# A decoder trunk on one core: the activation of a pass's last unit moved to VectorE, the residual prepared behind its read-back, output products in single steps, and more turned K tiles

## The chip, the core and the metric

The kernel runs on one core of a Trainium2 chip. The core has a matrix engine (TensorE, "PE" in the profile; its weight loads are "PEld"), a vector engine (VectorE, "DVE"), an activation engine (ScalarE, "ACT"), GpSimd ("POOL", used here to issue a few transfers) and SyncE ("SP", which issues all weight loads). The metric is the device time of one execution in microseconds.

## The reference

Two decoder layers over 256 positions of width 2048, in float32. Layer 0 mixes with a gated short convolution, layer 1 with multi-head latent attention; both are followed by the same kind of MLP, and every sub-layer ends in a normalisation of a scaled residual:

```python
def sq_relu_mlp(x, w1, w2):
    return jnp.square(jax.nn.relu(x @ w1)) @ w2

    for layer in range(DEPTH):                       # DEPTH = 2, N_A = 1
        if layer < N_A:
            mix = short_conv_mixer(h, ...)
        else:
            mix = mla_mixer(h, ...)                  # 16 heads, then o @ w_o
        h = layer_norm(ALPHA * h + mix, ...)
        h = layer_norm(ALPHA * h + sq_relu_mlp(h, mlp_w1[layer], mlp_w2[layer]), ...)
```

The MLPs (2048 to 8192 and back) are most of the arithmetic, and the change lies mainly in them.

## The kernel before

**Numbers in two parts.** Each float32 operand is split into hi and lo, both in the matrix engine's fast 32-bit type, and a product is hi·hi + lo·hi + hi·lo. A weight tile is loaded as `raw` (512 KB, SyncE), ScalarE casts it to `hi` (line 136), VectorE subtracts to get `lo` (line 137). An activation tile holds its hi and lo halves side by side. So a product of one K tile is `high` (line 224: weight hi by 512 columns) and `low` (line 228: weight lo by 256 columns), and `whole` (lines 366 and 367) adds the two halves of the result: a copy on ScalarE, then an addition on VectorE. `mm_run` goes over the 16 K tiles in the order high, low; for the K tile numbered `turned` (2) it puts low ahead of high. `TURN(q, m)` says for which units that is done.

**The MLP in passes.** The 8192 hidden columns are done in eight passes `q` of 1024; a pass has eight units `m` of 128 columns (`ps_u`), each with all 16 K tiles. Passes 0 and 7 are plain. In passes 1 to 6 (`FAST`) the second matrix product uses seven products instead of eight on 2 by 2 blocks. Two units make a pair: their sums are written to the two halves of a tile `u` (`fp` in the profile), ScalarE applies Relu and Square to the whole of it once the second unit is there (line 730), `form` builds block sums in three VectorE instructions (lines 645, 646, 648), and a split (lines 136 and 137 again) writes the pair's left factors: `h1c` and `h1a` for the first MLP (pairs 0 and 1, and pairs 2 and 3 of a pass), `h3c` and `h3a` for the second. On the right, the weights of the second product are combined as well: `raw_t` (line 171) and two more instructions (175, 178) on VectorE make further tiles that are split like the rest.

**Order.** `steps` gives, per unit, the set of seven products (`ps`, 21 matmuls, lines 309, 311, 312) that follows it. It is delayed by `SHIFT` = 5 units: behind units 5, 6, 7 of a pass come the products of its pairs 0, 1, 2 with the first half of the outputs, behind unit 0 of the next pass those of pair 3, and then the four pairs with the second half. So the factors of pair 3, which need unit 7, are used after one more set of products and one more unit. When the first half is done, ScalarE copies seven sums out of the PSUM banks and seven others in (lines 620, 695).

**The residual.** `held_x` holds the input of the sub-layer. In the first MLP, `begin` prepares it for the next normalisation while pass 1 runs: chunk 0 behind half of pass 0's output blocks (`ps_d`), with a scaling (line 419), two matmuls that take its mean over the partitions (`mu0p`, line 421) and a copy; the other 15 behind units 0 to 4 of pass 1, one VectorE instruction each (line 426: scale, subtract). Each group of chunks is then written to DRAM (`parked`, line 738, five transfers from POOL's queue), since its place in SBUF is needed for `sums`. After pass 7's hidden units the chunks are read back (`xback`, line 761, four transfers), and `to_wide` adds the turned output blocks to them, counts the moments and casts (lines 512, 431 to 437, 453, 454) for the next products.

**The output projection of attention** starts while the last heads are still being finished: `out_first` issues the matmuls of three output blocks K tile by K tile, and `BEHIND` says how many of its steps follow each step of the heads.

**Who orders the work.** The code emits instructions in program order; a planner in the framework then fixes, when the kernel is built, the order of each engine's queue, by emission order and by when it estimates operands to be ready. In the trace an engine's order therefore differs from the order of emission: splits of later weights stand between instructions of one pair. Once fixed, each queue runs in order. Weights are prepared some steps ahead (`take`), in 7 raw buffers and 9 pairs of hi and lo.

Of the kernel before, what the change touches and what calls it, by code (L numbers as in the profile page):

```python
# [13 lines left out]
ALU = mybir.AluOpType  # L14
# [4 lines left out]
T = 256  # L19
D = 2048  # L20
NC = D // P
FF = 4 * D
NQ = 8
QC = FF // NQ // P
H = 16
# [9 lines left out]
NB = 4  # L35
BW = D // NB
FAST = range(1, NQ - 1)
SHIFT = 5


def TURN(q, m):
    return m == 0 or not (q == 1 and m < SHIFT or q == NQ - 1 and m > SHIFT)
FIRST = (0, 1, 2, 3, 4, 6, 8, 12, 16)
LEAD = 4
HEAD = 4
# [2 lines left out]
TURNED = 2  # L48
LAG = 8
WO_G = 3  # L50
BEHIND = (2, 2, 2, 3, 2, 2, 3)

C_G, C_B, C_CW, C_QG, C_KG, C_END = 0, 64, 128, 176, 180, 184

# [2 lines left out]
def trunk(ctx: ExitStack, tc: tile.TileContext, xT, vecs, lead, w_first, w_in, w_out, w_kv, w_q, w_uk, w_uv,  # L57
          w_qn, w_qp, w_o, w1, w2, w2f, cosT, sinT, mask, ident, gb, out):
    nc = tc.nc
# [11 lines left out]
    held_x = [xres]  # L71
    parked = ctx.enter_context(tc.tile_pool(name="parked", bufs=1, space=bass.MemoryType.DRAM)).tile(
        [P, NC, T], F32, tag="parked", name="parked")
# [136 lines left out]
    def psum(name, bank=None):  # L210

        bank = Banks.next() if bank is None else bank
        return (pmm if bank < 4 else Banks.more).tile([P, 512], F32, tag=f"mm{bank}", name=name)
# [8 lines left out]
    def high(ps, w, blk, x, first):  # L222

        nc.tensor.matmul(ps, w[blk // 8][0][:, blk % 8, :], x, start=first, stop=False)  # L224

    def low(ps, w, blk, x, last):

        nc.tensor.matmul(ps[:, :T], w[blk // 8][1][:, blk % 8, :], x[:, :T], start=False, stop=last)  # L228

    def mm_run(wps, x, k0, k1, nk, turned=None):  # L230

        for k, (w, ps) in [(k, u) for k in range(k0, k1) for u in wps]:
            if k == turned:
                low(ps, w, k, x[k], False)
            high(ps, w, k, x[k], k == 0)
            if k != turned:
                low(ps, w, k, x[k], k == nk - 1)
# [86 lines left out]
    def down(x, put, n, sums=None):  # L324

        ps = [sums[n, t] if sums else psum("ps_d") for t in range(2)]
        for j in range(len(x) // 2):
            w, = take(1)
            for kk in range(2):
                k = 2 * j + kk  # L330
                for t in range(2):
                    dot(ps[t], wide_rows(w, kk), held(x[k], t), k == 0 and not sums, k == len(x) - 1, onto=bool(sums))
        for t in range(2):
            put(n, t, ps[t])
# [190 lines left out]
    xhl = [t[:, k, :] for t in xts for k in range(NC // 2)]  # L525
# [17 lines left out]
    for k0, k1 in pieces:  # L543
        half, at = k0 // 8, slice(k0 % 8, (k1 - 1) % 8 + 1)
        xt = xts[half][:, at, :]
        x, w = sources[k0]
# [12 lines left out]
    for m in range(NC):  # L559
        part = []  # L560
        for what in "cub":
            ps = next(pss)
# [23 lines left out]
    def mlp(idx, ln, blocks, fast, begin=None, extra=None, last=False):  # L586
# [5 lines left out]
        xhl = [xt[:, k, :] for k in range(NC)]  # L592
# [57 lines left out]
        def finish_pair(j, u):  # L650
            f = factors[j // 2][:, j % 2]
            if q in FAST:
                form(u)
                split(f[:, 0, :], f[:, 1, :], u[:, P:])
            else:
                split(f[:, 0, :2 * T], f[:, 1, :2 * T], u[:, :2 * T])

        q = 0
        for m in range(QC):
            if m < GROUP:  # L660
# [5 lines left out]
                ps = ws[m][1]  # L666
            else:
                ws = [(take(), psum("ps_w"))]
                mm_wide(ws, ln.xd)
                ps = ws[0][1]  # L670
# [4 lines left out]
        acc = act.tile([P, 2, D], F32, tag="a1", name=f"acc{idx}")  # L675
        for n in range(NB):
            down(h, put, n)
            if begin and n == 1:
                begin(range(1), (Banks.count + 4) % 8)

        base = Banks.count
        bank = {p: (base + i) % 8 for i, p in enumerate(("6", "unit", "3", "1", "5", "7", "2", "4"))}
# [2 lines left out]
        ps, onto, fresh = {}, set(), set()  # L685
# [30 lines left out]
        for q, m, pair in steps():  # L716
            lone = pair is None
            if q == FAST[0] and m == SHIFT:
                for o, _, _ in FACTORS:
                    resume(o, 1)  # L720
            w = take(2, 7)
            at = "6" if lone and m % 2 == 0 else "unit"
            un = psum("ps_u", bank[at])
            mm_run([(w, un)], xhl, 0, NC, NC, turned=TURNED if TURN(q, m) else None)
            if m % 2 == 0:
                u = fast.tile([P, 8 * P], F32, tag="fp", name="fp")
            whole(un, u[:, (m % 2) * T:(m % 2 + 1) * T])
            if m % 2:
                for function in (AF.Relu, AF.Square):
                    nc.scalar.activation(u[:, :2 * T], u[:, :2 * T], function)  # L730
                if m > 1 or lone:
                    finish_pair(m // 2, u)
            if extra and q == FAST[0] and m < NB:
                for t in range(2):
                    extra(block, m, t, spare[1 + (2 * m + t) % 3])
            if begin and q == FAST[0] and m < SHIFT:
                begin(range(3 * m + 1, 3 * m + 4))
                nc.gpsimd.dma_start(parked[:, 3 * m + (m > 0):3 * m + 4, :], held_x[0][:, 3 * m + (m > 0):3 * m + 4, :])
            if q == FAST[0] and m == SHIFT:
                sums = act.tile([P, 4, 2, BW], F32, tag="xres", name=f"sums{idx}")  # L740
            if q == NQ - 1:
                for _ in range(3 if m >= SHIFT else 2):
                    next(folds, None)
            if pair:
                products_of(*pair)
            if m == 1 and not lone:
                finish_pair(0, u)
            if q == NQ - 1 and last and m >= QC - 2:
                for t in range(2):
                    last_sum(m - QC + 2, t, spare[2 * (m - QC + 2) + t])  # L750
# [14 lines left out]
    def to_wide(block, put, h):  # L765

        def turned(n):
            for c in range(2):
                ps = psum("turned")
                for j in range(4):  # L770
                    src = block(n, j % 2)[:, (2 * c + j // 2) * P:(2 * c + j // 2 + 1) * P]
                    nc.tensor.transpose(ps[:, j * P:(j + 1) * P], src, id_t)
                summed(ln, [ps[:, j * T:(j + 1) * T] for j in range(2)], add, 4 * n + 2 * c)

        ln.widen("b")
        for n in range(NB):
            down(h, put, n)
            if n:
                turned(n - 1)
        ln.ws = group_of(GROUP)  # L780
        mm_wide(ln.ws, ln.xd, 0, NC - 4)
        turned(NB - 1)
        mm_wide(ln.ws, ln.xd, NC - 4)
# [3 lines left out]
    def prepare_chunks(chunks, bank=None):  # L787
        for k in chunks:
            ln.prepare(k, bank)
# [5 lines left out]
    with tc.tile_pool(name="att", bufs=1) as ap:  # L795
# [68 lines left out]
        for m in range(NK):  # L864
            ps = next(pss)
# [16 lines left out]
        oT = [ot[:, k, :] for k in range(H)]  # L882
# [6 lines left out]
        with tc.tile_pool(name="att2", bufs=2) as a2, \  # L889
# [83 lines left out]
            first_o = []  # L973
            after = Norm(2, ALPHA)

            def out_first():

                for i in range(WO_G):
                    first_o.append((take(), psum("ps_wo")))
                for k in range(H):  # L980
                    mm_run(first_o, oT, k, k + 1, H)
                    after.prepare(k)
                    yield

            boxes = [{} for _ in range(4)]
            for _ in project(0, boxes[0]):
# [1 line left out]
            for g in range(1, 4):  # L988
# [5 lines left out]
                for _ in items:  # L994
                    pass
            outs = out_first()
            for s, n in enumerate(BEHIND, H - 4):
                together(s)
# [178 lines left out]
```

## Time and profile before

| | |
|---|---|
| median of 3 runs | 2008.79 us (2006.48 to 2009.18) |
| profiled execution | 2009.8 us, span 2007.7 us |
| TensorE busy | 1990.3 us (99%) |
| VectorE busy | 1719.5 us (86%) |
| ScalarE busy | 1291.6 us (64%) |
| mean granted TensorE clock | 0.998 |
| read from HBM | 383.87 MB |

The passes of the first MLP lie between about 380 and 1060 us of the span, those of the second between about 1330 and 1998. A timeline row is: start, duration, engine, line, operation, output and inputs, shapes, count, and in brackets the idle time of the engine ahead of it with what ended it. Durations of queued instructions overlap by some tenths of a microsecond, so the pace is read from the distance of starts. A row of the waits is: who waited for whom, total us, times, longest.

### The profile page before, as it was taken

The numbers are of one execution on the slowest core, as the hardware profiler recorded it, in microseconds if no ns is written. First come the engines' busy times: TensorE is split into PE (matmuls) and PEld (weight loads), VectorE is DVE, ScalarE is ACT, GpSimd is POOL, SyncE is SP. The second block draws the span as 40 slices with busy tenths as digits, with TensorE's granted clock in tenths as the row PEclk, the third lists the DMA queues.
The fourth block names the chain that finished last, engine by engine and source line by source line (L and its number), as shares of the span: only waits on it lengthen the run. The fifth ranks groups of instructions, "written<-read, shape, count | busy, mean of one in ns | idle before, by whom it ended". The sixth has DMA issues, their size and how long they took to land.

```text
span 2007.7 us, 29769 instructions
## 1 busy us (share of the span) xinstructions
PE 1990.3 (99%) x11062; PEld 1733.5 (86%) x11062; DVE 1719.5 (86%) x2493; ACT 1291.6 (64%) x1914; POOL 7.3 (0%) x30
## 2 busy tenths in 40 slices
PE   9999999999999999999999999999999999999998
PEld 8888888988888888888889998898888888888886
DVE  8667677798899999999988988778989999999995
ACT  7444445586667767677756655557676776767772
POOL 0000000000000000000000000000000000000000
PEclk9999999999999999999999999999999999999999
DMA  9666666575565565655764543656556556665572
GB/s 344 210 192 186 189 188 192 182 223 157 195 212 175 202 210 190 211 186 202 261 218 153 182 138 131 185 187 181 165 171 210 190 190 208 207 212 181 198 261 95
DMA packets 107888, 390.00 MB, mean 194 GB/s; under 512 B 12000, under 2 KB 12768, under 8 KB 107488
## 3 DMA queue, kind: packets, MB, share of 16 engines
q1 hardware_dynamic: 106560, 383.79, 58.8%
q0 software_dynamic: 1040, 4.19, 0.6%
q8 instruction: 86, 1.41, 0.3%
q14 instruction: 58, 0.48, 0.1%
q10 hardware_dynamic: 144, 0.13, 0.0%
HBM read 383.87 MB, written 4.19 MB: 193 GB/s over the span
## 4 chain that ended last, share of the span: by engine, by line
PE 87%; DVE 8%; issue 3%; DMA 1%; ACT 1%; DVEq 0%; ACTq 0%
PE ps_u L224 16%; PE ps_l L224 13%; PE ps_u L228 8%; PE ps_l L228 7%; PE ps L312 6%; PE ps L309 6%; PE ps L311 6%; DVE lo L137 3%; PE ps_d L309 2%; PE ps_d L312 2%; PE ps_d L311 2%; PE ps_w L258 2%; PE ps_w L257 2%; PE ps_w L256 2%; DVE raw_t L171 1%
## 5 line engine op out<-in xcount | busy, mean ns | idle before, releaser
L137 DVE TENSOR_TENSOR lo<-raw,hi 128x1024 fp32r<-128x1024 f32 x710 | 855.3, 1218 | 175.8 <-ACT hi L136 105.7
L136 ACT CAST hi<-raw 128x1024 fp32r<-128x1024 f32 x710 | 735.5, 1054 | 223.3 <-PE ps_l L224 103.6
L224 PE MATMUL ps_u<-xhl,hi 128*128 128x512 f32 x1792 | 620.6, 393 | 0.0
L228 PE MATMUL ps_u<-xhl,lo 128*128 128x256 f32 x1792 | 485.4, 280 | 0.0
L224 PEld LDWEIGHTS ps_u<-xhl,hi 128*128 128x128 f32 x1792 | 329.0, 187 | 66.5 <-issue 0.3
L228 PEld LDWEIGHTS ps_u<-xhl,lo 128*128 128x128 f32 x1792 | 338.0, 189 | 12.8
L224 PE MATMUL ps_l<-xhl_a,hi 128*128 128x512 f32 x704 | 244.1, 393 | 0.0
L228 PE MATMUL ps_l<-xhl_a,lo 128*128 128x256 f32 x704 | 195.4, 279 | 0.0
L136 ACT CAST hi_t<-raw_t 128x1024 fp32r<-128x1024 f32 x96 | 101.5, 1058 | 133.5 <-DVE raw_t L171 126.1
L224 PEld LDWEIGHTS ps_l<-xhl_a,hi 128*128 128x128 f32 x704 | 132.1, 188 | 29.9
L228 PEld LDWEIGHTS ps_l<-xhl_a,lo 128*128 128x128 f32 x704 | 131.9, 188 | 0.2
L171 DVE TENSOR_TENSOR raw_t<-raw,raw 128x1024 f32<-128x1024 f32 x96 | 116.8, 1217 | 10.6 <-DMA raw<-in_w2f_dram 10.6
L137 DVE TENSOR_TENSOR lo_t<-raw_t,hi_t 128x1024 fp32r<-128x1024 f32 x96 | 116.9, 1218 | 1.1 <-ACT hi_t L136 1.0
L366 ACT COPY t<-ps_u 128x256 f32<-128x256 f32 x112 | 41.5, 371 | 89.7 <-PE ps_u L228 89.5
L224 PE MATMUL ps_l<-z,hi 128*128 128x512 f32 x240 | 82.4, 391 | 0.0
L730 ACT ACTIVATE fp<-fp 128x512 f32<-128x512 f32 x112 | 71.5, 638 | 8.8 <-DVE fp L367 8.1
L258 PE MATMUL ps_w<-xd,hi 128*128 128x258 f32 x256 | 72.7, 284 | 0.0
L224 PE MATMUL ps_l<-oT,hi 128*128 128x512 f32 x208 | 72.6, 398 | 0.0
L256 PE MATMUL ps_w<-xd,hi 128*128 128x258 f32 x256 | 72.3, 282 | 0.0
L257 PE MATMUL ps_w<-xd,lo 128*128 128x258 f32 x256 | 72.3, 282 | 0.0
L178 DVE TENSOR_TENSOR raw<-raw 128x512 f32<-128x512 f32 x96 | 66.2, 690 | 2.4
L175 DVE TENSOR_TENSOR raw<-raw,raw_t 128x512 f32<-128x512 f32 x96 | 65.7, 684 | 1.0
(349 smaller groups left out, 3878.4 us busy)
## 6 DMA issues: line engine op xcount, KB each, us to landing
raw<-in_w_dram SPq DMA_DIRECT2D x320, 512.0 KB, 4.2
raw<-in_w2f_dram SPq DMA_DIRECT2D x192, 512.0 KB, 5.2
raw<-in_w_in_dram SPq DMA_DIRECT2D x88, 512.0 KB, 3.7
raw<-in_w_out_dram SPq DMA_DIRECT2D x32, 512.0 KB, 4.2
raw<-in_w_o_dram SPq DMA_DIRECT2D x32, 512.0 KB, 4.1
raw<-in_w_kv_dram SPq DMA_DIRECT2D x10, 512.0 KB, 4.4
raw<-in_w_q_dram SPq DMA_DIRECT2D x8, 512.0 KB, 4.0
raw<-in_w_uk_dram SPq DMA_DIRECT2D x8, 512.0 KB, 4.2
```

The source lines that it names most:

```text
L136: nc.scalar.copy(hi, src)
L137: nc.vector.tensor_tensor(lo, src, hi.bitcast(F32), ALU.subtract)
L171: nc.vector.tensor_tensor(t.rearrange(two, a=2), b12.unsqueeze(1).to_broadcast([P, 2, BW]), r1.rearrange(two, a=2), ALU.subtract)
L224: nc.tensor.matmul(ps, w[blk // 8][0][:, blk % 8, :], x, start=first, stop=False)
L228: nc.tensor.matmul(ps[:, :T], w[blk // 8][1][:, blk % 8, :], x[:, :T], start=False, stop=last)
L256: nc.tensor.matmul(ps[:, :W], hi, x[k][:, :W], start=k == 0, stop=False)
L257: nc.tensor.matmul(ps[:, :W], lo, x[k][:, :W], start=False, stop=False)
L258: nc.tensor.matmul(ps[:, :W], hi, x[k][:, W:], start=False, stop=k == NC - 1)
L309: nc.tensor.matmul(ps, x[0], w[0], start=first, stop=False, skip_group_check=onto)
L311: nc.tensor.matmul(ps[:, at], x[0], w[1][:, at], start=False, stop=False, skip_group_check=onto)
L312: nc.tensor.matmul(ps, x[1], w[0], start=False, stop=last, skip_group_check=onto)
L730: nc.scalar.activation(u[:, :2 * T], u[:, :2 * T], function)
```

## The change

Four edits.

1. In passes 1 to 6, units 6 and 7 of a pass are activated separately. For unit 6 ScalarE applies Relu and Square to its 256 columns as soon as its sum is there. For unit 7 VectorE does both in one instruction, max(u, 0) · u.
2. `begin` no longer prepares the residual during passes 0 and 1. The chunks are written out as they are, in two transfers of eight chunks behind units 0 and 2 of pass 1. `to_wide` prepares four chunks behind each output block, after they have been read back; the bank of `mu0p` is now the next in turn.
3. `out_first` yields behind every single matmul rather than behind every K tile, and `BEHIND` is given in matmuls: six times the old numbers, except that one matmul moves from the sixth place to the fifth.
4. In the second MLP, units 1 to 4 of pass 1 get a turned K tile too.

```diff
-def TURN(q, m):
-    return m == 0 or not (q == 1 and m < SHIFT or q == NQ - 1 and m > SHIFT)
+def TURN(q, m, extra):
+    return m == 0 or not (q == 1 and m < SHIFT or q == NQ - 1 and m > SHIFT) or extra and q == 1 and m <= NB
...
-BEHIND = (2, 2, 2, 3, 2, 2, 3)
+BEHIND = (12, 12, 12, 18, 13, 11, 18)
...
             down(h, put, n)
-            if begin and n == 1:
-                begin(range(1), (Banks.count + 4) % 8)
...
-            mm_run([(w, un)], xhl, 0, NC, NC, turned=TURNED if TURN(q, m) else None)
+            mm_run([(w, un)], xhl, 0, NC, NC, turned=TURNED if TURN(q, m, extra) else None)
...
-            if m % 2:
+            late = q in FAST and m >= QC - 2
+            if late and m % 2:
+                nc.vector.scalar_tensor_tensor(u[:, T:2 * T], u[:, T:2 * T], 0.0, u[:, T:2 * T], ALU.max, ALU.mult)
+            elif late or m % 2:
                 for function in (AF.Relu, AF.Square):
-                    nc.scalar.activation(u[:, :2 * T], u[:, :2 * T], function)
-                if m > 1 or lone:
-                    finish_pair(m // 2, u)
+                    at = u[:, :T] if late else u[:, :2 * T]
+                    nc.scalar.activation(at, at, function)
+            if m % 2 and (m > 1 or lone):
+                finish_pair(m // 2, u)
...
-            if begin and q == FAST[0] and m < SHIFT:
-                begin(range(3 * m + 1, 3 * m + 4))
-                nc.gpsimd.dma_start(parked[:, 3 * m + (m > 0):3 * m + 4, :], held_x[0][:, 3 * m + (m > 0):3 * m + 4, :])
+            if begin and q == FAST[0] and m < 4:
+                if m % 2 == 0:
+                    nc.gpsimd.dma_start(parked[:, 4 * m:4 * m + 8, :], held_x[0][:, 4 * m:4 * m + 8, :])
...
         for n in range(NB):
             down(h, put, n)
+            prepare_chunks(range(4 * n, 4 * n + 4))
             if n:
                 turned(n - 1)
...
                 for k in range(H):
-                    mm_run(first_o, oT, k, k + 1, H)
-                    after.prepare(k)
-                    yield
+                    for i, (w, ps) in enumerate(first_o):
+                        high(ps, w, k, oT[k], k == 0)
+                        yield
+                        low(ps, w, k, oT[k], k == H - 1)
+                        if i == WO_G - 1:
+                            after.prepare(k)
+                        yield
```

## The prediction

> **What bounds the kernel now.** I read the page's head first, then who kept TensorE waiting.
>
> ```profile
> span 2007.7 us, 29769 instructions
> PE 1990.3 (99%) x11062; PEld 1733.5 (86%) x11062; DVE 1719.5 (86%) x2493; ACT 1291.6 (64%) x1914; POOL 7.3 (0%) x30
> ```
>
> ```profile
> PE ps L309 <- ACT h1a L136: 3.4, 4, 1.1
> PE ps L309 <- ACT h3a L136: 3.2, 3, 1.1
> PE ps L312 <- DVE h3a L137: 2.1, 1, 2.1
> PE ps L312 <- DVE h1a L137: 1.9, 1, 1.9
> ```
>
> TensorE is the bound: 17.4 us of the span are not its own, and 10.6 of them are these four rows (engine and line that waited, for whom: us, times, longest). All nine waits are for one kind of thing: the split left factors of a pair of hidden units (h1a in the first MLP, h3a in the second; hi from ScalarE, lo from VectorE). Nothing waits for weights or for a transfer. So the fast passes are where time can be had, and only at those places. They show in the timeline as units or products that last too long:
>
> ```profile
> 754.56 0.39 PE L224 MATMUL ps_u<-xhl,hi 128*128 128x512 f32 x1
> ...
> 760.12 0.39 PE L309 MATMUL ps<-hi,h1a 128*128 128x512 f32 x1
> ...
> 764.93 0.39 PE L224 MATMUL ps_u<-xhl,hi 128*128 128x512 f32 x1
> ...
> 771.65 0.50 PE L309 MATMUL ps<-hi,h1a 128*128 128x512 f32 x1 [1.00 <-ACT h1a L136]
> ...
> 1884.64 0.39 PE L224 MATMUL ps_u<-xhl,hi 128*128 128x512 f32 x1
> ...
> 1891.47 0.50 PE L309 MATMUL ps<-hi,h3a 128*128 128x512 f32 x1 [1.10 <-ACT h3a L136]
> ```
>
> A unit normally takes 760.12 - 754.56 = 5.56 us and a set of seven products 764.93 - 760.12 = 4.81. The unit at 764.93 takes 6.72, the one at 1884.64 takes 6.83: **short stops** of 1.16 and 1.27 us, first and last of six, one before the last products of the pass's first half in passes 4, 5 and 6 of both MLPs. The **long stops** stand at the end of pass 1 in each MLP:
>
> ```profile
> 517.85 0.50 PE L309 MATMUL ps<-hi,h1a 128*128 128x512 f32 x1 [0.24 <-ACT h1a L136]
> 520.45 0.50 PE L312 MATMUL ps<-hi,h1a 128*128 128x512 f32 x1 [1.87 <-DVE h1a L137]
> 521.85 0.63 PE L309 MATMUL ps<-hi_t,h1a 128*128 128x512 f32 x1
> 522.27 0.63 PE L311 MATMUL ps<-lo_t,h1a 128*128 128x512 f32 x1
> 526.49 0.39 PE L224 MATMUL ps_u<-xhl,hi 128*128 128x512 f32 x1
> ...
> 1469.02 0.39 PE L309 MATMUL ps<-hi,h3a 128*128 128x512 f32 x1
> ...
> 1477.78 0.40 PE L224 MATMUL ps_u<-xhl,hi 128*128 128x512 f32 x1
> ```
>
> These products take 8.64 and 8.76 us for 4.81. The stop itself is about 2 us; after it matmuls start 0.42 us apart (521.85 to 522.27), nearly twice the usual step.
>
> **Part 1, the last unit's activation.** Why the factors are late shows in a short stop, on VectorE and ScalarE:
>
> ```profile
> 846.66 0.42 DVE L367 TENSOR_TENSOR fp<-ps_u,t 128x256 f32<-128x256 f32 x1
> ...
> 851.00 0.28 DVE L645 TENSOR_TENSOR fp<-fp 128x128 f32<-128x128 f32 x1
> ```
>
> ```profile
> 849.35 0.63 ACT L730 ACTIVATE fp<-fp 128x512 f32<-128x512 f32 x1
> ...
> 853.98 1.05 ACT L136 CAST hi_t<-raw_t 128x1024 fp32r<-128x1024 f32 x1 [3.06 <-DVE raw_t L171]
> 854.93 0.93 ACT L136 CAST h1a<-fp 128x896 fp32r<-128x896 f32 x1
> ```
>
> The unit's sum is written at 846.66. Its start and the start of form (line 645) at 851.00 are 4.3 us apart; 4.0 of them lie behind the sum's own 0.3. In between the pair is on ScalarE for two activations (the second at 849.35), and the planner has filled VectorE's queue with weight splits, which are not over when the activations are. On ScalarE the factor's cast at 854.93 stands behind a cast that sat idle for 3.06 us until raw_t came. The factor is there at 854.93 + 0.93 = 855.86. TensorE, stopped for 1.1 to 1.3 us in such a place, would have used it near 854.6 (855.86 less 1.27).
>
> After the change the first unit's half is activated one unit earlier, and the second by one VectorE instruction:
>
> ```profile
> L426 DVE SCALAR_TENSOR_TENSOR xres<-xres,mu x30: 411/414/421, 160.0 to 447.7; 128x256 f32<-128x256 f32 x30
> ```
>
> The nearest row for it is the two-input 128x256 instruction, 0.41 us. Sum, instruction, form are now one chain on VectorE. If the planner again slips one split of 1.2 us (3.48 / 3, row at 510.81 below) into each link, form begins 1.2 + 0.4 + 1.2 = 2.8 us after the sum for 4.0, which gains 1.2 us; and if raw_t falls behind form, the cast no longer stands behind hi_t and 0.95 us more is gained (853.98 to 854.93). Lowest 1.2, highest, without any slipped in, 4.0 - 0.4 = 3.6. A short stop is 1.16 to 1.27, so I take all six as gone: mean 1.22 x 6 = **7.3 us**. What is late next is the lo half, wanted two steps of 4.81 / 21 = 0.23 us after hi.
>
> ScalarE loses 12 x 2 instructions of 0.63 us on 512 columns (849.35) and gains 12 x 2 on 256 columns one unit earlier, where 5.56 us of unit and 4.81 of products still follow: nothing on the path, and less work than before. VectorE gains 12 x 0.41 = 5 us, hidden by its idle time:
>
> ```profile
> 604.62:687.56 82.94, 82.94 (x427) 70.67 (x425) 78.48 (x96) 58.99 (x82) 0.00 (x0) 1.00 0.59 203
> 771.65:855.91 84.26, 83.16 (x424) 70.66 (x424) 79.71 (x97) 60.28 (x83) 0.00 (x0) 1.00 0.58 200
> ```
>
> (The stretch, its length, then busy us of PE, PEld, DVE, ACT, POOL, clock, DMA.) A pass without a stop is 82.94 us; VectorE works 79.7 in a pass with one. With 0.41 more and no stop it has 82.94 - 80.1 = 2.8 us left. If that cover were gone, the 5 us would be paid in full.
>
> **The long stops** have another reason for lateness:
>
> ```profile
> 510.81 3.48 DVE L137 TENSOR_TENSOR lo<-raw,hi 128x1024 fp32r<-128x1024 f32 x3
> ...
> 516.69 0.68 DVE L137 TENSOR_TENSOR t<-raw,t 128x512 fp32r<-128x512 f32 x1
> 518.17 1.23 DVE L171 TENSOR_TENSOR raw_t<-raw,raw 128x1024 f32<-128x1024 f32 x1 [0.80 <-DMA raw<-in_w2f_dram]
> 519.31 1.08 DVE L137 TENSOR_TENSOR h1a<-fp,h1a 128x896 fp32r<-128x896 f32 x1
> ```
>
> ```profile
> 516.86 0.94 ACT L136 CAST h1a<-fp 128x896 fp32r<-128x896 f32 x1
> ```
>
> VectorE stands at raw_t until a transfer lands at 518.17, and the factor's lo half is queued behind it. Lo needs the cast of hi, done at 516.86 + 0.94 = 517.80; raw_t's turn came when t was done, near 517.3. So lo was ready half a microsecond too late for the planner to put it first. Here three splits (510.81, 3.48 us) stand between sum and form; with two links instead of three the chain is 3.48 / 3 = 1.16 us less 0.41, so 0.75 us, shorter, and lo goes ahead of raw_t. In the first MLP the residual's work also leaves this pass. With less than half a microsecond gained the stop stays. Bounds 0 and (8.64 - 4.81 + 0.24) + (8.76 - 4.81) = 8.0 us. I take **8.0**, since half a microsecond decides and the edit moves the order that way, and keep 0 for the range.
>
> [...] The granted clock of the pass behind the first long stop is the last column but two:
>
> ```profile
> 517.30:601.40 84.10, 81.99 (x408) 68.98 (x407) 77.49 (x93) 57.99 (x76) 0.00 (x0) 0.98 0.59 199
> ```
>
> It is 0.98, while the two passes above have 1.00: with the 0.42 us steps this says that the clock fell behind a stop of 2 us. [...] What the slow steps are worth is 3.83 - 1.87 = 2.0 us in the first case and 3.95 - 2.1 = 1.85 in the second, 3.8 together.
>
> **Part 2, the residual.** Sixteen prepare instructions of 0.41 us, with mu0's matmuls, leave pass 0 and pass 1 of the first MLP and come behind the read-back; the write-out becomes two transfers for five on POOL's queue, the same bytes, earlier.
>
> ```profile
> 430.54 0.59 PE L421 MATMUL mu0p<-xres,ones 128*128 128x256 f32 x2
> 430.78 0.59 PE L309 MATMUL ps_d<-hi,h 128*128 128x512 f32 x1
> ...
> 999.90 1.64 POOL L761 DMA_DIRECT2D xback<-parked  x3 [550.18 <-DVE fp L367]
> 1007.15 0.54 POOL L761 DMA_DIRECT2D xback<-parked  x1 [5.62 <-issue]
> ...
> DMA to landing us min/median/max: 6.9/8.1/11.0
> ...
> 1012.75 1.22 DVE L137 TENSOR_TENSOR lo<-raw,hi 128x1024 fp32r<-128x1024 f32 x1 [1.49 <-ACT hi L136]
> 1013.95 0.39 PE L312 MATMUL ps_d<-hi,h1a 128*128 128x512 f32 x1
> ```
>
> mu0's two matmuls cost TensorE 0.24 us (430.54 to 430.78) and the longer matmul behind them 0.2 (0.59 for 0.39): 0.4 us, which leave pass 0 and come back behind the first output block, whose last matmul starts at 1013.95. There mu0 wants the first four chunks, landed at 999.90 + 6.9 = 1006.8, and one scaling on VectorE: some 6.9 us of cover. If that were gone, TensorE would stop for it, since its own queue is in order. Behind the scaling on VectorE stand weight splits, and TensorE waits for those; but VectorE sat idle 1.49 us ahead of one of them in this stretch, so the 16 x 0.41 = 6.6 us find room in a few such gaps, and the chunks are wanted only when the first turned block is added, a block later. The fourth read-back is issued at 1007.15, so there by 1018.2 at the slowest; its chunks are added last, after three more blocks. On POOL's queue nothing stands behind the write-out until 999.90. mu0 now takes the next bank in order, so the later blocks use banks shifted by one of eight. Taken: 0; bounds +2 (mu0 late by as much as a long stop) and -0.4 (not paid again).
>
> **Parts 3 and 4.** The output products keep their 96 steps; one of them moves ahead of a head's step in TensorE's order. 0, with bounds of 0.2 either way, which is what a change of kind costs once (0.59 for 0.39 at 430.78). Turning swaps two neighbouring matmuls in four units and adds none; the trace has no such unit of the same place in both forms, so the bound is a change of kind in each, 4 x 0.2 = 0.8 either way. With no row for either sign I take 0.
>
> **Sum.** 2009.8 (profiled execution) - 7.3 - 8.0 = 1994.5. That execution is 1.0 above the median of the three runs, 2008.8, so against it **1993.5**.
>
> **The rivals.** (a) A long stop stays, since raw_t keeps its place: 1997.5 with one, 1993.5 + 8.0 = 2001.5 with both. For it: lo misses by half a microsecond, the gain is about as much. (b) The slow steps have another cause than the stop and stay: 1993.5 + 3.8 = 1997.3. For it: the stop is short, 1.87 us; against it: the clock of 1.00 in passes without one. [...] (c) The planner fills the new links so that the short stops stay and the long go: 1993.5 + 7.3 = 2000.8; if none goes, 2008.8, no change. (d) Slower: VectorE is the real bound of the passes, and the stop is only where its lateness shows. Then each instruction added lengthens the pass: 12 x 0.41 = 5 us, 2013.8. For it: 79.7 of 84.26 us busy. Against it: a pass with 78.48 busy runs in 82.94 without a stop. It decides once VectorE's free time in a pass is under the 1.2 us that TensorE gets faster and the 0.41 added; it is 84.26 - 79.71 = 4.55.
>
> **How the numbers follow.** Forecast 0.45; (a) 0.28; (b) 0.03; (c) 0.05 and 0.07 for none; (d) 0.12. 0.2% (4 us) is about what a measurement tells from no change. Faster: 0.45 + 0.28 + 0.03 + 0.05 = 0.81; same 0.07; slower 0.12. Range: below, the lowest run 2006.5 less 15.3, and 0.7 for the bounds of parts 2 to 4, of which hardly all fall on one side: 1990.5; above, (a) with both long stops and 1 us of small costs: 2002.5. Outside are none, (d): 0.19.
>
> **What would show it.** Right: the four waits for h1a and h3a gone or under 0.3 us each; units before the last products at 5.56; no products of 8 us; PE's clock at 1.00 in pass 2; mu0's matmuls near 1014 without a wait. Wrong: a stop at 517 or 1469 with raw_t still ahead of the factor's lo; a new wait of TensorE for lo of the weights (VectorE the bound); a wait for mu0 or xback.

## The result and the profile after

The changed kernel takes 2001.24 us (median of 6 runs, 1998.02 to 2002.59) against 2008.99 for the kernel before (6 runs beside it, 2005.68 to 2010.59): ratio 0.9962, 95% interval 0.9949 to 0.9975, 7.75 us faster. The forecast was 1993.5, the range 1990.5 to 2002.5. The time lies in the range, by its upper end, where rival (a) with both long stops stood (2001.5); half of the gain is missing. The profiled execution took 2002.59 us, span 2000.7, against 2009.8 and 2007.7.

The page's busy lines and the waits of TensorE after the change:

```profile
PE 1988.5 (99%) x11062; PEld 1732.5 (87%) x11062; DVE 1720.3 (86%) x2505; ACT 1289.0 (64%) x1914; POOL 5.6 (0%) x27
```

```profile
PE ps L312 <- DVE h1a L137: 2.2, 1, 2.2
PE ps_d L312 <- DVE h1a L137: 1.2, 1, 1.2
PE ps L312 <- DVE h3a L137: 1.1, 1, 1.1
PE ps L309 <- ACT h1a L136: 0.7, 1, 0.7
```

The rows of 3.4 and 3.2 us for ScalarE's half of the factors, the short stops, are gone. Left are the long stop of the first MLP (2.2 and 0.7), a smaller one at the place of the second (1.1), and a new one in an output block behind pass 7 (ps_d, 1.2). By the starts of units and products the two profiled executions differ as follows:

| place | before | after | difference |
|---|---|---|---|
| the six units with a short stop behind them | 40.8 | 33.4 | -7.4 |
| six other units of these passes, 5.61 to 5.68 for 5.57 (each now behind 26 or 27 product matmuls in a row for 21, since the planner has moved some ahead) | 33.4 | 33.9 | +0.5 |
| long stop, first MLP: unit and products | 5.97 + 8.64 | 6.54 + 10.04 | +2.0 |
| long stop, second MLP: products | 8.76 | 6.18 | -2.6 |
| first output block behind pass 7 | 10.9 | 12.46 | +1.6 |
| output projection, 416 matmuls of ps_l | 73.48 | 72.14 | -1.3 |
| everything else | | | +0.2 |
| span | 2007.7 | 2000.7 | -7.0 |

VectorE at the end of pass 1 of the first MLP, before (the unit's sum, the first and the last instruction of form) and after the change (a timeline; in brackets the idle time of the engine ahead of the row):

```profile
510.47 0.42 DVE L367 TENSOR_TENSOR fp<-ps_u,t 128x256 f32<-128x256 f32 x1
...
514.21 0.28 DVE L645 TENSOR_TENSOR fp<-fp 128x128 f32<-128x128 f32 x1
...
516.49 0.28 DVE L648 TENSOR_TENSOR fp<-fp 128x128 f32<-128x128 f32 x1
```

```profile
507.89 1.23 DVE L171 TENSOR_TENSOR raw_t<-raw,raw 128x1024 f32<-128x1024 f32 x1 [1.94 <-DMA raw<-in_w2f_dram]
...
511.38 0.42 DVE L367 TENSOR_TENSOR fp<-ps_u,t 128x256 f32<-128x256 f32 x1
...
512.84 0.42 DVE L728 SCALAR_TENSOR_TENSOR fp<-fp 128x256 f32<-128x256 f32 x1
...
514.32 0.28 DVE L645 TENSOR_TENSOR fp<-fp 128x128 f32<-128x128 f32 x1
...
517.12 0.28 DVE L648 TENSOR_TENSOR fp<-fp 128x128 f32<-128x128 f32 x1
...
519.11 1.22 DVE L171 TENSOR_TENSOR raw_t<-raw,raw 128x1024 f32<-128x1024 f32 x1 [1.10 <-DMA raw<-in_w2f_dram]
520.26 1.08 DVE L137 TENSOR_TENSOR h1a<-fp,h1a 128x896 fp32r<-128x896 f32 x1
```

```profile
517.49 0.94 ACT L136 CAST h1a<-fp 128x896 fp32r<-128x896 f32 x1 [4.99 <-DVE fp L648]
```

From the sum to the start of form there are 2.94 us for 3.74 before: 0.80 shorter, near the 0.75 that the prediction worked out. But form itself, from its first instruction to its last, takes 2.80 us for 2.28, since the planner now slips a second weight split (1.22 us) between its instructions where line 178 (0.68 us) stood. So the whole chain is only 0.28 us shorter (5.74 for 6.02). The sum itself comes 0.91 us later than before, since VectorE has waited 1.94 us for 1.03 at its raw_t near 507 for an earlier transfer. At the end nothing has changed places: hi, which lo needs, is done at 517.49 + 0.94 = 518.43, raw_t's turn comes near 518.0, and so raw_t still stands ahead of the factor's lo and waits for its own transfer.

### The profile page after: what moved, and what is told of

The parts are those of the page before. It is cut to its first block, busy times and chain, and to the rows that moved or that the text cites. A ratio compares the mean times of both kernels' runs of the same rounds, so it can differ in the third digit from the quotient of the medians.

```text
span 2000.7 us, 29698 instructions
## 1 busy us (share of the span) xinstructions
PE 1988.5 (99%) x11062; PEld 1732.5 (87%) x11062; DVE 1720.3 (86%) x2505; ACT 1289.0 (64%) x1914; POOL 5.6 (0%) x27
## 4 chain that ended last, share of the span: by engine, by line
PE 95%; DMA 2%; DVE 1%; issue 1%; ACT 0%; SPq 0%; DVEq 0%; POOLq 0%; ACTq 0%
PE ps_u L224 20%; PE ps_l L224 13%; PE ps_u L228 10%; PE ps L312 7%; PE ps L311 7%; PE ps L309 7%; PE ps_l L228 7%; PE ps_d L312 2%; PE ps_d L309 2%; PE ps_d L311 2%; PE ps_w L258 2%; PE ps_w L257 2%; PE ps_w L256 2%; DMA raw<-in_w2f_dram 1%; PE ps_g L258 1%; PE ps_g L256 1%
## 5 line engine op out<-in xcount | busy, mean ns | idle before, releaser
L732 ACT ACTIVATE fp<-fp 128x512 f32<-128x512 f32 (+1 forms) x112 | 65.9, 588 | 7.2 <-DVE fp L367 6.8
```

## The experiments

My theory after the traces: (1) the short stops ended by the early activation; (2) the long stops are the order "raw_t, then lo" on VectorE, with a transfer that lands at different times; (3) the new stop is the scaling of the residual, which waits at the head of VectorE's queue; (4) the 1.3 us of the output projection belong to the one matmul that moves. The rival to (1) and (2) was that VectorE has too much work in these passes.

### Parts alone: p1, p2, p34, no2

p1 is the kernel before with the activation alone, p2 with the residual alone, p34 with the output products' order and the turned tiles; no2 is the changed kernel without the residual's move. The edits are the hunks of the diff above.

> The kernel before with the separate activation of units 6 and 7 alone (part 1). Theory: the six short stops go by this alone, 7.3 us; the long stop at the end of pass 1 of the first MLP stays, since raw_t still stands ahead of the factor's lo on VectorE (products there 8 to 10.5 us instead of 4.81), and the one of the second MLP shrinks to a wait of about 1.3 us without a lower clock (products about 6.2, 2.6 us less). No wait near 1010. So 7.3 + 2.6 = 9.9 us less than before, less up to 2 if the first long stop gets worse: ratio 0.9955, 0.9945 to 0.9965. Rival: the gain of the changed kernel's passes needs the other parts (VectorE without the residual in pass 1); then some short stops stay, or the long stop is still longer, and the ratio is over 0.997.

p1 measured 2000.82 us, ratio 0.9970 (0.9959 to 0.9981). No short stop is left; in the profiled execution the second long stop is as long as before (products of 8.73 us). Its waits for the factors:

```profile
PE ps L312 <- DVE h1a L137: 2.2, 1, 2.2
PE ps L312 <- DVE h3a L137: 1.9, 1, 1.9
```

So part 1 does what it should at the six places, alone, and the 0.9970 is near what these are worth (7 of 2008 us). The second half of my expectation fell: part 1 does not shrink the second long stop.

> The kernel before with the residual prepared behind its reading back alone (part 2). Theory: a new wait of about 1.2 us for the lo of h1a near 1010, where the scaling of the chunks waits for the transfer at the head of VectorE's queue with the last pair's lo behind it; everything else as before: all six short stops and both long stops (8.6 and 8.8 us). Time 1.5 to 2 us above before, ratio 1.0008 (1.0000 to 1.0015). Rival (the value of the prediction): the part costs nothing, and taking the residual's 15 instructions out of pass 1 lets the lo at 519 come earlier: first long stop under 1 us, 2 to 4 us less than before, ratio 0.998 to 0.999.

p2 measured 2006.78 us, ratio 0.9991 (0.9982 to 1.0001). The new wait is there but smaller (the first output block takes 11.41 us for 10.9, since the read-back landed after 4.06 us of waiting for 5.11), both sets of short stops and the first long stop are as before (6.90 + 8.15). The second long stop, in code that p2 does not touch, was 6.24 us for 8.76. The price of the part is below what the ratio can tell.

> The kernel before with the order of the first output products and the turned tiles alone (parts 3 and 4). Theory: the output projection (416 matmuls into ps_l) takes 72.1 us instead of 73.5, since the one moved matmul changes the rhythm of the starts behind it (three pairs of matmuls in 1041 instead of 1060 ns); the turned tiles change at most 0.1 us; stops as before. Ratio 0.9993 (0.9988 to 0.9998). Rival (the prediction): 0 within 0.8 us, and the 1.3 us seen in the changed kernel came with something else, such as its shifted banks; then the output projection stays at 73.5.

p34 measured 2006.48 us, ratio 0.9993 (0.9983 to 1.0002). The stretch of the output projection (start and end, length, busy us of PE, PEld, DVE, ACT, clock, DMA), before and in p34:

```profile
1237.48:1310.96 73.48, 73.48 (x416) 63.67 (x416) 10.00 (x24) 0.00 (x0) 1.00 0.60 182
```

```profile
1238.52:1310.66 72.14, 72.14 (x416) 63.54 (x416) 10.00 (x24) 0.00 (x0) 1.00 0.60 186
```

So the gain belongs to part 3 (p1 and p2 have 73.48 and 73.47, no2 72.14). The second long stop was nearly absent. Part 4 touches this pass, but only TensorE's order in its earlier units. VectorE there, before and in p34:

```profile
1469.66 1.22 DVE L171 TENSOR_TENSOR raw_t<-raw,raw 128x1024 f32<-128x1024 f32 x1 [1.80 <-DMA raw<-in_w2f_dram]
1470.81 1.08 DVE L137 TENSOR_TENSOR h3a<-fp,h3a 128x896 fp32r<-128x896 f32 x1
```

```profile
1467.62 1.21 DVE L171 TENSOR_TENSOR raw_t<-raw,raw 128x1024 f32<-128x1024 f32 x1
1468.76 1.08 DVE L137 TENSOR_TENSOR h3a<-fp,h3a 128x896 fp32r<-128x896 f32 x1
```

The same order; before, raw_t waits 1.80 us for its transfer, in p34 it finds it there. In all these kernels raw_t stands ahead of the lo. Over eight executions its wait and what the products took beyond 4.80 us go together: 0 and 0.4 (p34), 0.30 and 1.4 (p2), 0.69 and 1.6 (pinB, below), 0.94 and 1.4 (the changed kernel), 1.27 and 3.9 (p1), 1.43 and 3.9 (scal, below), 1.48 and 2.2 (no2), 1.80 and 4.0 (before). The order is not strict, for two reasons that the traces show: behind the three stops of about 4 us the granted clock halved (0.50 over the 3.40 us from 1473.40 in the kernel before), and behind the others it did not (1.00 over the 3.40 us from 1470.80 in the changed kernel and from 1470.90 in pinB); and in the five kernels with the early activation (the changed one, p1, scal, no2, pinB) a weight split of 1.13 us stands between raw_t and the lo as well. That the same kernel differs from one execution to the next shows in its clock. Of the 44 runs of the kernel before that were taken beside these experiments, 8 have a mean granted clock of 1.000 (2005.61 to 2006.80 us), 26 of 0.999 and 10 of 0.998 (2008.85 to 2011.36). One stretch of 3.4 us at half clock lowers the mean by 0.0008 (1.7 of 2008 us), and the profiled execution, with one behind each long stop, has 0.998. The 2.6 us that this place gave in the profiled pair are thus, as far as these runs tell, the landing of a transfer in one execution, and no part of the change earned them: p1 has the stop in full.

> The changed kernel with the residual's preparation put back where it was (parts 1, 3 and 4). Theory: the wait near 1010 goes (1.2 us, with the slowed matmuls behind it 1.5), the short stops stay gone, the first long stop stays as in the changed kernel (raw_t first), since the residual's instructions in pass 1 were not what held the lo. 1.5 us under the changed kernel: ratio to before 0.9955 (0.9945 to 0.9965). Rival: the residual's leaving pass 1 helped there; then the first long stop is longer than in the changed kernel's and the sum is no better than it, 0.9962 or above.

no2 measured 2000.52 us, ratio 0.9965 (0.9953 to 0.9978). No wait behind pass 7, short stops gone, first long stop 6.25 + 8.96 us: the residual's instructions in pass 1 were not what held the lo. The second was 7.03. As a ratio it cannot be told from the changed kernel's.

### The order of the queue: pinA, pinB, pinC, pin0

Instructions emitted under `issue_after(x)` are queued behind x: in pinA raw_t starts at 518.82, behind the factor's lo at 516.48, and in the changed kernel at 519.11, ahead of the lo at 520.26. `split` returns its VectorE instruction for that.

pinA:

```diff
+                latest[0] = split(f[:, 0, :], f[:, 1, :], u[:, P:])
...
-                products_of(*pair)
+                with tc.issue_after(latest[0].ins) if q == 2 and m == 0 else ExitStack():
+                    products_of(*pair)
```

> The changed kernel with one thing pinned in both MLPs: the preparation that is emitted with the products behind pass 1's last pair (raw_t and what follows it) is queued on VectorE behind that pair's lo. Theory: what makes TensorE stop at 517 and 1469 is that lo stands behind raw_t, which waits for a transfer whose landing differs from execution to execution (VectorE waited for it 1.8, 0.3, 0, 0.9, 1.3 and 1.5 us at the second place in six executions, and the stop there was the longer the longer this wait). With lo first, lo ends near 518.3 and TensorE wants it near 518: the first stop falls from 6.2 us (with its slow steps) to 0.5 or less and the second from 1.3 to 0, with no window of a lower clock. 6 to 7 us under the changed kernel: ratio to before 0.993 (0.9920 to 0.9940). The wait near 1010 stays, 1.2. Rival: the pass is short of weights there whatever the order; then raw_t, queued later, brings a stop at the next unit or products instead (a wait for hi or lo of a weight of 1 to 3 us within 40 us behind the place), and the ratio stays at 0.995 or above.

pinA measured 1995.38 us, ratio 0.9937 (0.9922 to 0.9952). VectorE at the first place:

```profile
515.12 0.29 DVE L648 TENSOR_TENSOR fp<-fp 128x128 f32<-128x128 f32 x1
516.48 1.09 DVE L137 TENSOR_TENSOR h1a<-fp,h1a 128x896 fp32r<-128x896 f32 x1 [1.06 <-ACT h1a L136]
...
518.82 1.22 DVE L171 TENSOR_TENSOR raw_t<-raw,raw 128x1024 f32<-128x1024 f32 x1
```

Lo goes first, at 516.48 for 520.26, and raw_t, whose turn comes at 518.82, no longer waits. The pin holds back more than raw_t: of these 3.8 us, 1.0 come from an earlier sum (510.40 for 511.38), 1.0 from a shorter chain from sum to last form (4.72 for 5.74), and 1.8 from the lo no longer standing behind raw_t. The products there take 5.51 us for 10.04, the second place has no stop, the clock has no low stretch (mean 1.000). Two small delays appear a pass and more later (products of 5.20 and a unit of 5.73 near 665): 0.6 us, the only sign of the rival.

pinB:

```diff
-            prepare_chunks(range(4 * n, 4 * n + 4))
+            with tc.issue_after(state["factor"]):
+                prepare_chunks(range(4 * n, 4 * n + 4))
```

> The changed kernel with the scaling of the first four chunks queued on VectorE behind the lo of the last pair of pass 7. Theory: the wait of 1.2 us near 1010 comes from the scaling, which stands at the head of VectorE's queue for 5.1 us until the read-back has landed, with that lo behind it; with lo ahead the first output block takes 10.9 us for 12.46, and mu0 (behind the block, near 1013) has no wait or one under 0.5. 1.5 us under the changed kernel: ratio to before 0.9955 (0.9940 to 0.9970), told by the length of the block rather than by the ratio. Rival: the lo is late whatever stands ahead of it, or mu0 now waits for the scaling as long as the lo did; then block and mu0 together are as long as in the changed kernel (12.7 us).

pinB measured 1999.18 us, ratio 0.9955 (0.9940 to 0.9970); the place itself decides. VectorE in the changed kernel and in pinB:

```profile
1009.74 0.29 DVE L419 TENSOR_SCALAR xback<-xback 128x256 f32<-128x256 f32 x1 [5.11 <-DMA xback<-parked]
1009.95 1.22 DVE L137 TENSOR_TENSOR lo<-raw,hi 128x1024 fp32r<-128x1024 f32 x1
1011.09 0.68 DVE L137 TENSOR_TENSOR h1a<-fp,h1a 128x512 fp32r<-128x512 f32 x1
```

```profile
1005.43 0.69 DVE L137 TENSOR_TENSOR h1a<-fp,h1a 128x512 fp32r<-128x512 f32 x1
1007.69 0.30 DVE L419 TENSOR_SCALAR xback<-xback 128x256 f32<-128x256 f32 x1 [1.57 <-DMA xback<-parked]
```

In the changed kernel the factor's lo stands behind an instruction that waits 5.11 us for a read-back. With lo ahead, the block takes 10.93 us for 12.46 and mu0 has no wait.

pinC is both pins, and in pass 1's last unit the same for the set of products emitted a unit earlier, which waits behind the end of form:

```diff
-                products_of(*pair)
+                with tc.issue_after((formed if q == 1 else latest)[0].ins) if (q, m) in ((1, 7), (2, 0)) else ExitStack():
+                    products_of(*pair)
```

> The two pins above together, and in pass 1's last unit nothing between sum, activation and form on VectorE: the preparation emitted with the unit before is queued behind form as well. Theory: the pins add up, and what pinA leaves of the first stop (the splits between the links, 3.6 us) goes too: no stop over 0.3 us at 517, 1469 and 1010. 8 to 9 us under the changed kernel: ratio to before 0.992 (0.9910 to 0.9930). Rival: splits that are held back by 3 us are late for TensorE, which then waits for lo of the weights in the next unit or products; then the ratio is that of pinA or worse.

pinC measured 1992.70 us, ratio 0.9923 (0.9907 to 0.9940). That is 8.5 us under the changed kernel's median, and 7.8 by the two ratios, since the runs of the kernel before beside it were 1.5 us faster than those beside the changed one. Its busy lines and all that TensorE still waits for:

```profile
PE 1984.1 (100%) x11062; PEld 1731.3 (87%) x11062; DVE 1720.9 (86%) x2505; ACT 1287.0 (65%) x1914; POOL 5.7 (0%) x27
```

```profile
PE ps_e L1077 <- ACT umeans L1075: 1.6, 1, 1.6
PE warm L383 <- DVE col L384: 1.1, 1, 1.1
```

No factor is late any more; what is left lies at the two ends of the program. It beats both kernels.

pin0 is the kernel before with pinA's pin and nothing else.

> The kernel before with the pin of pinA alone (raw_t and what follows queued behind the lo of pass 1's last pair), none of the four parts. Theory: the order in that place alone makes the two long stops, and part 1 had no share in them: both fall to 0.5 us or less (hi may still be 0.2 to 0.4 late in the first), the six short stops stay. 7 to 8 us under before in an execution in which both stops were long (8.6 and 8.8 us of products), less where the second was short: ratio 0.9967 (0.9955 to 0.9980). Rival: without part 1 the form comes too late in any order, a stop of 1.5 us or more stays in one of the two places, and the ratio is 0.998 or above.

pin0 measured 2005.14 us, ratio 0.9985 (0.9975 to 0.9994): less than I expected, and by the ratio the rival's. By the trace it is not the rival: no stop of 1.5 us stays. The long stops went as the theory has it (5.89 + 5.61 us at the first place, a wait of 0.2 at the second), and the short ones stayed:

```profile
PE ps L309 <- ACT h3a L136: 3.3, 3, 1.1
PE ps L309 <- ACT h1a L136: 3.3, 3, 1.1
PE ps L312 <- DVE h1a L137: 0.9, 2, 0.5
```

The size failed for two reasons: 1.6 us of new small delays a pass later (products of 5.59 and 5.33, units of 5.71 and 5.72), which the trace shows, and, going by the other executions, a second stop that costs the kernel before 4 us only now and then. All ten runs of pin0 have a mean clock of 1.000 and lie within 1.6 us of each other. So the order alone ends the long stops, and the activation is not needed for it.

### Is VectorE needed for the activation? scal

```diff
-            if late and m % 2:
-                nc.vector.scalar_tensor_tensor(u[:, T:2 * T], u[:, T:2 * T], 0.0, u[:, T:2 * T], ALU.max, ALU.mult)
-            elif late or m % 2:
+            if late or m % 2:
                 for function in (AF.Relu, AF.Square):
-                    at = u[:, :T] if late else u[:, :2 * T]
+                    at = u[:, (m % 2) * T:(m % 2 + 1) * T] if late else u[:, :2 * T]
```

> The changed kernel with the last unit's own half activated by ScalarE too (Relu and Square on 256 columns), so that only the early activation of the first half is left of part 1. Theory: what ends the short stops is that the planner, seeing a shorter way over ScalarE, slips in three instructions between sum and form (lo, t4, lo) instead of four, 1.2 us less; then VectorE's taking the activation is not needed: the six stops are gone or under 0.3 us, and the ratio is that of the changed kernel, 0.9962 (0.9950 to 0.9975). Rival: the hand-over to ScalarE and back is itself what makes the factor late; then stops of 0.5 us or more stay in passes 4 to 6, 3 us and more in all, and the ratio is 0.9977 or above.

scal measured 1999.69 us, ratio 0.9961 (0.9946 to 0.9976), and has none of the six short stops. VectorE from sum to form in a pass that had one, after the change and in scal:

```profile
846.42 0.42 DVE L367 TENSOR_TENSOR fp<-ps_u,t 128x256 f32<-128x256 f32 x1
846.75 0.68 DVE L175 TENSOR_TENSOR raw<-raw,raw_t 128x512 f32<-128x512 f32 x1
847.35 0.42 DVE L728 SCALAR_TENSOR_TENSOR fp<-fp 128x256 f32<-128x256 f32 x1
...
848.82 0.28 DVE L645 TENSOR_TENSOR fp<-fp 128x128 f32<-128x128 f32 x1
```

```profile
841.93 0.42 DVE L367 TENSOR_TENSOR fp<-ps_u,t 128x256 f32<-128x256 f32 x1 [0.51 <-ACT t L366]
...
844.73 0.29 DVE L645 TENSOR_TENSOR fp<-fp 128x128 f32<-128x128 f32 x1
```

2.4 us and 2.8 us, for 4.3 before. Activating the first half a unit earlier is enough to end the short stops, whichever engine does the second half. Whether VectorE's instruction would do it without the early half was not tried.

### One matmul: even

The kernel pinC with `BEHIND = (12, 12, 12, 18, 12, 12, 18)` for `(12, 12, 12, 18, 13, 11, 18)`.

> The kernel pinC with the output products in single steps, but twelve behind each of the two steps that have 13 and 11 in the changed kernel. Theory: the 1.34 us of the output projection come from the one matmul that is moved, which changes the distance of the starts behind it; without it the 416 matmuls into ps_l take 73.5 us again for 72.1. Rival: the finer steps themselves, or other instructions between, did it; then 72.1 stays. (Seen in the length of that stretch, not in the total.)

One execution, 1994.05 us. The stretch of the output projection in this kernel (the columns as above):

```profile
1229.57:1303.05 73.48, 73.48 (x416) 63.72 (x416) 10.03 (x24) 0.00 (x0) 1.00 0.58 183
```

73.48 us again: the single matmul that moves from the sixth place to the fifth earns the 1.34 us, in matmuls that all come behind it. All fourteen traces agree: 72.14 us in the nine kernels that move it, 73.47 or 73.48 in the five that do not.

### How much VectorE can take: load2 and load4

```diff
             split(hi, lo, tiled(raw))
+            if state.get('load') and i % 8 == 0:
+                nc.vector.tensor_tensor(lo, tiled(raw), hi.bitcast(F32), ALU.subtract)
```

(`i % 4` in load4; `state['load']` holds in passes 1 to 6.)

> The kernel pinC with the lo half of every eighth half weight tile of the fast passes subtracted twice on VectorE, 24 instructions more, 2 in a pass, each 1.14 us from start to start; the output is the same. Theory: VectorE is not the bound; it has 3.7 us a pass free (82.88 of which 79.15 busy, mean of three passes), so 2.3 more are hidden: time within 3 us of pinC, 1992 to 1996. Rival (VectorE bounds the passes, so each instruction added there lengthens its pass): 24 x 1.14 = 27 us more, 2020.

> The kernel pinC with the lo half of every fourth half weight tile of the fast passes subtracted twice, 48 instructions more, 4 in a pass; the output is the same. Theory: 4.6 us more in a pass for 3.7 free, so the free time is used up and 0.9 us a pass, 11 us in all, comes out on TensorE's side, with waits for lo of weights or factors in every pass: 2004 (1998 to 2015). Rival 1 (VectorE bounds the passes already): 48 x 1.14 = 55 us more, 2048. Rival 2 (idle time shown there isn't all usable, or busy time counts overlaps): still hidden, under 1998, or over 2015.

One execution each: load2 1997.42 us, 4.7 over pinC, a little over my 3; load4 2017.47, 24.8 over, twice what I expected and above its range. A pass of load4 (the columns as in the prediction) and its largest waits:

```profile
794.91:880.61 85.70, 84.18 (x427) 70.30 (x425) 84.10 (x102) 60.19 (x82) 0.00 (x0) 1.00 0.59 196
```

```profile
PE ps L313 <- DVE lo_t L137: 5.7, 8, 0.9
PE ps L311 <- ACT hi L136: 2.6, 3, 0.9
```

Of 27 us of extra VectorE work 4.7 came out, so VectorE does not bound the passes. Of 55 us, 24.8 came out: 30 were hidden, 2.5 us a pass. Already at 2.3 us a pass 0.4 came out, so rival 2 was right that not all of the 3.7 us that busy times give can be used. The added instruction also makes the lo that it writes again 1.14 us later, so a part of what came out may be that.

## Why the prediction was right or wrong

**The short stops (7.3 us): right**, in place, size and mechanism. All six went, in p1 alone and in scal; form begins 2.1 us behind the sum (2.4 from start to start) for the 2.8 worked out. What the prediction did not see is that VectorE's instruction is not needed for it (scal).

**The long stops (8.0 us): wrong, and this is the missing half.** The step that failed is "with two links instead of three the chain is 3.48 / 3 = 1.16 us less 0.41, so 0.75 us, shorter, and lo goes ahead of raw_t". The way to form did get 0.80 us shorter, but form itself got 0.52 longer, so 0.28 was left; lo was again ready some 0.4 us behind raw_t's turn, and raw_t kept its place. VectorE also waited longer for an earlier transfer (1.94 us at 507.89). The first stop grew by 2.0 us in the profiled pair. This is what the prediction itself gave as a sign of being wrong, a stop at 517 with raw_t still ahead of the factor's lo, and it is the mechanism of its rival (a). Behind the step lay a second mistake: I took the two stops of one execution for fixed lengths. The second follows the landing of a transfer, with 0 to 1.8 us of waiting over the executions above, and that execution, at a mean clock of 0.998, was like the slowest 10 of the 44 runs. So the 8.0 us were too much for a median run, whatever became of the order.

**The residual at 0: wrong by 1.6 us in the profiled pair**, inside the bound of 2 but by another way. The step that failed: "Behind the scaling on VectorE stand weight splits, and TensorE waits for those", with 6.9 us of cover for mu0. The cover was judged for the consumer of the transfer and not for what is queued behind the waiting instruction: the last pair's lo was. mu0 itself was never late. With pinB the part costs nothing, and with no2 it gains nothing.

**The output products at 0, bounds 0.2: wrong.** 1.34 us gained. I counted matmuls (the same 96 steps), and not the distances from start to start in the 416 behind them: 73.48 / 208 is 353 ns for a pair of high and low, 72.14 / 208 is 347.

**Turned tiles at 0, bounds 0.8: right.** Three units of pass 1 take 5.65 us for 5.63; units 4 and 5 together 11.27 for 11.19; 0.14 us lost.

**VectorE hidden (rival d): right**, by load2 and load4; where the prediction had 2.8 us free in a pass, 1.9 of 2.3 us added and 2.5 of 4.6 us added were hidden.

**The clock.** The granted clock right behind the long stops (the columns as in the prediction), before, and after the change at both places:

```profile
521.10:524.50 3.40, 3.40 (x10) 2.63 (x9) 2.50 (x4) 2.14 (x4) 0.00 (x0) 0.50 0.49 155
```

```profile
520.30:523.70 3.40, 2.31 (x6) 1.82 (x7) 3.40 (x6) 1.60 (x4) 0.00 (x0) 0.50 0.10 17
523.70:527.10 3.40, 3.40 (x9) 2.63 (x8) 1.45 (x2) 2.06 (x4) 0.00 (x0) 0.50 0.84 281
1470.80:1474.20 3.40, 3.17 (x14) 2.63 (x15) 2.84 (x5) 2.63 (x6) 0.00 (x0) 1.00 0.82 218
```

Half clock for 3.4 us behind the stop of 1.87 us before, for 6.8 us behind the one of 2.18 after (TensorE was idle for another 1.1 us in the first half of these), none behind the one of 1.09. In pinA and pinC, without the stop, it does not fall (mean 1.000 in both); rival (b) was wrong.

**Together.** Forecast gain 15.3 us, measured 7.75. In the profiled pair: short stops 7.4, output projection 1.3, second long stop 2.6 by the luck of a landing; less 2.0 and 1.6 for the two places where lo still stands behind a transfer, and 0.7 of small delays. That the time came out at the 2001.5 of rival (a) is luck in part: the first stop grew instead of staying, and the output projection, which no rival had, made up for most of the residual. With the two orders put right (pinC) the time is 1992.7, and no factor is late. That this lies so near the forecast is luck in part too, since 1.3 us of it are the output projection's.

## What to carry to other kernels

When an instruction waits for a transfer, look at what is queued behind it on the same engine, not at who reads the transfer: both places that cost time here were a ready factor behind a waiting instruction, and moving it ahead (in pinC, which also keeps weight splits out of the chain in front of it) gave about 8 us. The chain that became 0.28 us shorter here left the queue's order as it was; if the order is the cause, pin the order. And before a stop is counted as gain, see in a second execution whether it is there: one that follows the landing of a transfer was 0.4 us in one of these executions and 4 us in another, with VectorE's queue in the same order.

## What was not expected of the hardware

- **Matmuls of the same kind ran at two paces.** A pair of 512 and 256 columns took 353 ns from start to start (73.48 us for 208 pairs, the kernel before and even) or 347 (72.14 us, the changed kernel and p34), over the whole stretch, and one matmul moved ahead of them made the difference. What sets the pace was not found.
- **Of two stops of nearly the same length one had a lower clock behind it.** p2 and scal had nearly the same first stop (waits of 0.98 and 1.36 us, and of 1.00 and 1.32). The stretch right behind it, in p2 and in scal (the columns as in the prediction):

```profile
521.00:524.40 3.40, 3.40 (x10) 2.57 (x10) 2.39 (x4) 2.25 (x5) 0.00 (x0) 0.52 0.54 158
```

```profile
520.90:524.30 3.40, 3.40 (x17) 2.77 (x16) 3.13 (x5) 3.28 (x7) 0.00 (x0) 1.00 0.50 140
```

The mean granted clock is 0.52 behind p2's and 1.00 behind scal's, with 10 matmuls against 17 in the same 3.40 us. So the length of the stop alone did not decide it here; what did was not shown.

- **Why the transfer lands when it does** at the end of pass 1 was not tried; the pins only make it not matter.
